# Roots ahead of the norms, scale and bias on GpSimd, gates' product freed, and gathers cut into steps, in a two-layer diffusion backbone

## The chip, the cores and the metric

The kernel runs on one NeuronCore of one Trainium2 chip. The metric is the device time of one launch in microseconds (us), the median of three runs. The engines are TensorE (PE; its weight loads are shown apart as PEld), VectorE (DVE), ScalarE (ACT), GpSimd (POOL) and the DMA queue that SyncE issues (SP).

## The reference

One inference step of a backbone with two layers, width 1024, on 128 prompt tokens and 128 sample tokens. Each layer is:

```
h = x*(1+scale1)+shift1                # scale, shift, gate from SiLU(cond) @ w_ada
y = mixer(h)                           # one projection in; HGRN2 and mLSTM branches, both directions;
                                       # their gates; y = (sig(gA)*(yA@WA) + sig(gB)*(yB@WB)) @ W_out
x = LayerNorm(alpha*x + gate1*y)       # ((x-mu)*rsqrt(var+eps))*g + b
h = x*(1+scale2)+shift2
f = SwiGLU(h), width 2816  (layer 0);  top-2-of-8 mixture of SwiGLU experts, width 2816  (layer 1)
x = LayerNorm(alpha*x + gate2*f)
```

All matrices are fp32. There are four norms. The first three are followed by a modulated copy (layer 0's feed-forward, layer 1's mixer, layer 1's experts); "inner norms" are the first and the second, whose g and b the change touches.

## The kernel before, in words

**Products.** Each weight tile is read by DMA into a staging tile (`ws`, in the expert stage also `mws`), ScalarE casts it to its high part (`wh`, `mwh`), VectorE subtracts to get the low part (`wl`, `mwl`), and TensorE makes three products: high by high, low by high, high by low. Activations are split the same way (`hTh` and `hTl`). `split` does this for the dense stages; it also holds back the low part of a few tiles with `held`, until work of the norm has been issued. Nearly every matrix product is recorded under line 56, nearly every two-input VectorE operation under line 52, so groups are told apart by tile names.

**Modulation.** `ada_quad` multiplies the conditioning (`actT`) with tiles of w_ada (`wa`, two slots) into the bank `adq`. Most of the 48 quads are spread over the two mixers and the feed-forward by the list `todo`, and stand between blocks of other products.

**A norm.** `residual` adds the gated product to x in halves of 512 columns; `layer_norm` takes the statistics of one block of 128 tokens, `inverse_dev` takes a root on ScalarE (line 400) and one Newton step on VectorE (line 402), and a scaled subtraction on VectorE (line 469) leaves the normalised block in `z`, without g and b. `modulate` turns `z` through TensorE (line 414) and scales it on ScalarE (line 420) or, for one quarter, on VectorE (line 423); g and b of the norm are folded into this scale and bias. `hT_part` splits the result. `between` puts a quad of the modulation between the transposes of the two blocks. Only the next residual needs x itself, so `affine` makes x = z*g + b later: two VectorE instructions for each block and each half, 8 for each inner norm. In the first norm they are entries of `todo`, in the second they follow the split of the activations; both are tied to `last_split`. The rows g and b of the second norm (`nrow`) lie in the two slots of `wa`.

**The mixer's gates.** `gates` in `mixer` loads 32 columns of weights (`gwh`, `gwl`) and multiplies them with the activations; its first product is tied behind a place noted in `grow["after"]`.

**The experts.** They run in pairs (`experts`). For each pair `gather` picks the tokens by a product with a 0/1 matrix `sel`: four steps of 16 products, for two row blocks each, then ScalarE copies the bank to `xh` and VectorE subtracts into `xl` (line 1388), then TensorE turns `sel` in four transposes. xh and xl have one pair of buffers, so the new tokens overwrite those that the running pair reads. Gathers 1 to 3 are called between the first two matrices of an odd expert and its third one, and each step takes a bank from `bank`, which has three buffers and serves the experts' products; `gbank` is one bank more, used for transposes of the activations (line 1452).

**Order.** The instructions of each engine stand in the order that a planner gives them from a simulated timeline of its own. `tc.high_priority()` lifts what is inside it, `tc.issue_after(i)` keeps what is inside it behind instruction i.

**Stages on the profiled run, us.** Layer 0 mixer to 422; product out and first norm to 452; feed-forward to 650; second norm to 663; layer 1 mixer to 1044; product out and third norm to 1080; router and first gather to 1089; experts to 1893; last norm to 1911.

Of the kernel before, what the change touches and what calls it, by code (L numbers as in the profile page):

```python
# [41 lines left out]
def backbone(ctx, tc, x_prompt, x_sample, c, state_hgrn, state_mlstm_C, state_mlstm_n, state_mlstm_m,  # L42
# [22 lines left out]

    eps = const.tile([128, 1], F32, name="eps")
    V.memset(eps, LN_EPS)
    ident = const.tile([128, 128], F32, name="ident")
# [123 lines left out]

    staged = []
    held = []

    def split(st, shape):
        hi = wp.tile(shape, F32R, tag="wh", name="wh", bufs=3)
        S.copy(hi, st)  # L198
        lo = wp.tile(shape, F32R, tag="wl", name="wl", bufs=3)
        with tc.issue_after(held.pop(0)) if held else nullcontext():  # L200
            tt(lo, st, hi.bitcast(F32), ALU.subtract)
        return hi, lo
# [122 lines left out]
    def ada_quad(l, c4, kt, halves=None):  # L325
# [5 lines left out]
        for g in (2, 3, 0, 1):  # L331
            with tc.high_priority(), tc.issue_after(end) if g < 2 else nullcontext():
                end = mm(ps[32 * g:32 * g + 32], actT[:, kt, :], halves[g // 2][:, g % 2], kt == 0, kt == KT - 1,
                         (0, 32 * g))
# [45 lines left out]
    def rsqrt(pool, src, n, mul, eps):  # L380
# [12 lines left out]
        return y  # L393

    def inverse_dev(pool, var):

        v = pool.tile([128, 1], F32, tag="rs_v", name="rs_v", bufs=2)
        y = pool.tile([128, 1], F32, tag="rs_y", name="rs_y", bufs=2)
        t = pool.tile([128, 1], F32, tag="rs_t", name="rs_t", bufs=2)
        act(t, var, AF.Sqrt, bias=eps)  # L400
        V.tensor_scalar(v, var, -0.5, -0.5 * LN_EPS, op0=ALU.mult, op1=ALU.add)
        V.reciprocal(y, t)
        V.tensor_scalar(t, y, y, v, op0=ALU.mult, op1=ALU.mult)
        V.tensor_scalar(y, t, 1.5, y, op0=ALU.add, op1=ALU.mult)
        return y

    def modulate(src, gs, bs, hm, between):

        for tr in range(2):
            for q4 in range(2):  # L410
# [6 lines left out]
                for k in range(4):  # L417
                    kt = q4 * 4 + k
                    if not tr or q4:
                        last_act[:] = [act(hm[:, kt, tr], ps[:, k], AF.Identity, bias=bs[:, kt, tr:tr + 1],  # L420
                                           scale=gs[:, kt, tr:tr + 1]).ins]
                    else:
                        last_mod[:] = [V.tensor_scalar(hm[:, kt, tr], ps[:, k], gs[:, kt, tr:tr + 1],
                                                       bs[:, kt, tr:tr + 1], op0=ALU.mult, op1=ALU.add).ins]
# [3 lines left out]
    def modulated_parts(pool, tag, src, gs, bs, between=lambda end: keep_warm(12, end)):  # L428
# [3 lines left out]
        lo = ht.tile([128, KT, 256], F32R, tag="hTl", name="hTl", bufs=1)  # L432
        modulate(src, gs, bs, hm, between)
        for q in range(4):
            hT_part(hm, hi, lo, q)
        return [(hi[:, k], lo[:, k]) for k in range(KT)]

    def hT_part(hm, hi, lo, q):
        s = slice(2 * q, 2 * q + 2)
        f = hm[:, s].rearrange("p k r t -> p (k r t)")  # L440
        S.copy(hi[:, s].rearrange("p k t -> p (k t)"), f)
        last_split[:] = [V.tensor_tensor(lo[:, s].rearrange("p k t -> p (k t)"), f,
                                         hi[:, s].bitcast(F32).rearrange("p k t -> p (k t)"), op=ALU.subtract).ins]

    last_split = []

# [38 lines left out]

    def affine(dst, src, gb, tr, q4):

        o = slice(512 * q4, 512 * q4 + 512)
        tt(dst[:, tr, o], src[:, tr, o], gb[0][:, o], ALU.mult)
        tt(dst[:, tr, o], dst[:, tr, o], gb[1][:, o], ALU.add)  # L490

    QUARTERS = [(tr, q4) for tr in range(2) for q4 in range(2)]


    def mixer(l, rhs, mx, sm, hp, mp, quads):
# [13 lines left out]
        def gates():  # L509
            gh, gl = load_gate_w(W)  # L510
            pg = mp.tile([32, 256], F32, tag="mp", name="pg")
            for kt in range(KT):
                rh, rl = rhs[kt]
                with nullcontext() if kt else tc.issue_after(grow.pop("after")):
                    mm(pg, gh[:, kt], rh, kt == 0, False)
# [447 lines left out]
    def mix_out(l, mrhs, pool, tags, obank, spare, bufs=1):  # L963
        z, ng = x, None
        if l == 0:
            z = slot8([128, 2, D], "z")
        banks = [gemm_tm(w_out[l], 512 * q4, 512, mrhs, obank, 1 + 3 * q4, spare) for q4 in range(2)]
        with tc.issue_after(staged[0]):
# [93 lines left out]
    with ExitStack() as es:  # L1062
# [16 lines left out]
        for i in range(1, KT):  # L1079
            todo.append((1, 0, i))  # L1080
        def late_affine(tr, q4, z=z, ng=ng):
            with tc.issue_after(last_split[0]):
                affine(x, z, ng, tr, q4)

        todo += [lambda tr=tr, q4=q4: late_affine(tr, q4) for tr, q4 in QUARTERS]
        keep_warm(4)

# [4 lines left out]
        with tc.high_priority():  # L1092
            rhs = modulated_parts(fx, "hm", z, gs, bs, between)
        held[:] = [last_mod[0], last_split[0], last_split[0]]
        gTh = fx.tile([128, 22, 256], F32R, name="gTh")
        gTl = fx.tile([128, 22, 256], F32R, name="gTl")

        for f0 in range(0, DFF, 512):
# [6 lines left out]
            for i, b in enumerate(gemm_fm(ffn_w3[0], f0, n, rhs, bank=fbank)):  # L1105
                s = slice(f0 // 128 + 2 * i, f0 // 128 + 2 * i + 2)
                t_ = ts[i]
                tt(t_, t_, b, ALU.mult)
                S.copy(gTh[:, s], t_)
                tt(gTl[:, s], t_, gTh[:, s].bitcast(F32), ALU.subtract)  # L1110
        gb = gate_rows(fx, "gb", 0, 1)
        ng = [norm_row(wp, "wa", ap, 2) for ap in (ln2_g[0], ln2_b[0])]
# [16 lines left out]
    def hT1(mx):  # L1129
        with tc.high_priority():  # L1130
            parts = modulated_parts(mx, "AQ", z, gs, bs)
        held[:] = [last_mod[0], last_split[0], last_split[0]]
        with tc.issue_after(last_split[0]):
            for tr, q4 in QUARTERS:
                affine(x, z, ng, tr, q4)
        return parts
# [218 lines left out]
    def experts(first_slot):  # L1355
# [5 lines left out]
        def gather(p2):  # L1361
# [12 lines left out]
            if not first_slot and p2 == 0:  # L1374
                banks = [pe.tile([128, 2, 256], F32, tag="acc", name="acc", bufs=3) for _ in range(3)]
                banks.append(adp.tile([128, 2, 256], F32, tag="ad", name="acc"))
                for k2, ps in zip(range(0, KT, 2), banks):
                    part(ps, k2, hh, True, False)
            for k2 in range(0, KT, 2):
                if banks:  # L1380
                    ps = banks[k2 // 2]
                else:
                    ps = bank([128, 2, 256])
                    part(ps, k2, hh, True, False)
                part(ps, k2, hl, False, True)
                o = slice(k2, k2 + 2)
                S.copy(xh[:, o], ps)
                done = V.tensor_tensor(xl[:, o], ps, xh[:, o].bitcast(F32), op=ALU.subtract).ins  # L1388
            ps = gbank([128, 2, 2, 128])
            for tr in range(2):  # L1390
                for i in range(2):
                    PE.transpose(ps[:, i, tr], sel[:, tr, i].bitcast(F32), ident)
            selT = ms.tile([128, 2, 2, 128], F32R, tag="selT", name="selT", bufs=2)
            S.copy(selT, ps)
            return sel, selT, xh, xl, done

# [11 lines left out]
        if not first_slot:  # L1408
            with tc.issue_after(nxt[4]):
                V.tensor_reduce(most, pm, axis=AX.X, op=ALU.max)  # L1410
                V.tensor_copy(most_i, most)
            behind.append(nxt[4])
            late.append(nc.values_load(most_i[0:1, 0:1], min_val=0, max_val=256))
        for p2 in range(NE // 2):
            sel, selT, xh, xl, _ = nxt
            for i in range(2):
# [41 lines left out]
                if i and p2 + 1 < NE // 2:  # L1458
                    nxt = gather(p2 + 1)
                if e == NE - 1:  # L1460
                    out = ms.tile([128, 2, D], F32, tag="e8", name="out", bufs=2)
                for q4 in range(2):
                    o = slice(512 * q4, 512 * q4 + 512)
                    yb = bank([128, 512])
                    for kt, wh, wl in blocks([moe_w2[0, e]], 22, 512 * q4, 512):
                        gh, gl = gT[kt]
                        mm(yb, gh, wh, kt == 0, False)
# [65 lines left out]
```

## Time and profile before

| what | value |
| --- | --- |
| time, median of 3 runs | 1909.88 us (1909.39 to 1910.23) |
| the profiled execution | 1913.11 us, its span 1911.4 us |
| mean granted TensorE clock | 0.990 of full speed |
| PE busy | 1842.6 us (96%) |
| PEld busy | 1572.2 us (82%) |
| DVE busy | 1473.4 us (77%) |
| ACT busy | 1187.9 us (62%) |
| POOL busy | 21.3 us (1%), 51 instructions |
| DMA | 500.88 MB, mean 262 GB/s |

The span runs from the first to the last instruction of the core; the time of an execution also has what lies around it. Busy times include waits inside a pipelined instruction only as far as the profile models them. A full granted clock is 2.4 GHz; a share of 0.5 is the other level, 1.2 GHz, and values between are means over a stretch.

### The profile page before, as it was taken

What the parts mean: (1) busy time and instruction counts of PE and PEld (TensorE: products, weight loads), DVE (VectorE), ACT (ScalarE), POOL (GpSimd) and SP (SyncE); (2) the same over time, 40 slices, a digit from 0 to 9 for tenths busy, and PEclk for the clock granted to TensorE, in tenths of its full rate; (3) what the DMA queues carried; (4) which work ended last, traced back from release to release, by engine and by line L of the source; (5) the groups of instructions that cost most, each with busy time, mean ns of one, the idle gap of its engine ahead of it and who ended that gap; (6) DMA issues with size and microseconds to landing.
All of it is one profiled execution on the core that took longest, in us unless ns stands there. A gap on an engine that the chain in (4) does not pass through costs nothing.

```text
span 1911.4 us, 30874 instructions
## 1 busy us (share of the span) xinstructions
PE 1842.6 (96%) x11846; PEld 1572.2 (82%) x11846; DVE 1473.4 (77%) x2179; ACT 1187.9 (62%) x1531; POOL 21.3 (1%) x51
## 2 busy tenths in 40 slices
PE   7999999998999899999999999999999999999996
PEld 4877889996998688788999787888887888788884
DVE  3587598676455658869957798989888898889887
ACT  4547555644444445665564587777776777677773
POOL 0000000000000000000000000000000000000000
PEclk9999999999999999999999999999999999999998
DMA  9866845567756585775555989999998999999993
GB/s 315 259 228 203 269 142 160 157 198 277 230 170 194 162 286 194 244 220 149 149 161 172 361 297 346 363 323 366 349 349 312 358 350 343 307 350 352 348 342 128
DMA packets 273579, 500.88 MB, mean 262 GB/s; under 512 B 17044, under 2 KB 56552, under 8 KB 273424
## 3 DMA queue, kind: packets, MB, share of 16 engines
q1 hardware_dynamic: 273424, 498.83, 78.0%
q8 instruction: 95, 1.56, 0.3%
q14 instruction: 60, 0.49, 0.1%
HBM read 493.45 MB, written 5.32 MB: 261 GB/s over the span
## 4 chain that ended last, share of the span: by engine, by line
PE 83%; DMA 9%; DVE 3%; ACT 2%; issue 1%; SPq 1%; DVEq 0%; ACTq 0%
PE mm L56 62%; PE fp L56 9%; DMA wa<-in_w_ada_dram 6%; PE adq L56 2%; PE pl L56 2%; PE acc L56 1%; PE pn L56 1%; DMA ws<-in_ffn_w_dram 1%; DVE wl L52 1%; PE g L1452 1%; DVE mwl L52 1%; PE pqk L56 1%; DMA ws<-in_w_in_dram 1%; PE po L56 1%; ACT wh L198 1%
## 5 line engine op out<-in xcount | busy, mean ns | idle before, releaser
L52 DVE TENSOR_TENSOR mwl<-mws,mwh 128x1024 fp32r<-128x1024 f32 x432 | 516.8, 1223 | 52.3 <-ACT mwh L1319 48.3
L1319 ACT CAST mwh<-mws 128x1024 fp32r<-128x1024 f32 x432 | 445.8, 1052 | 117.1 <-PE mm L56 109.1
L52 DVE TENSOR_TENSOR wl<-ws,wh 128x1024 fp32r<-128x1024 f32 (+1 forms) x275 | 331.4, 1207 | 189.9 <-ACT wh L198 184.8
L198 ACT CAST wh<-ws 128x1024 fp32r<-128x1024 f32 (+1 forms) x275 | 284.7, 1036 | 308.8 <-PE mm L56 149.1
L56 PE MATMUL mm<-hTh,wh 128*128 128x256 f32 x1024 | 293.8, 289 | 4.6 <-ACT wh L198 2.5
L56 PE MATMUL mm<-hTl,wh 128*128 128x256 f32 x1024 | 293.0, 287 | 1.7 <-DVE hTl L52 1.0
L56 PE MATMUL mm<-hTh,wl 128*128 128x256 f32 x1024 | 291.7, 288 | 2.4 <-DVE wl L52 2.4
L56 PE MATMUL mm<-mwh,xh 128*128 128x512 f32 x704 | 278.8, 396 | 0.0
L56 PE MATMUL mm<-mwl,xh 128*128 128x512 f32 x704 | 277.5, 399 | 0.9 <-DVE mwl L52 0.8
L56 PE MATMUL mm<-mwh,xl 128*128 128x512 f32 x704 | 278.4, 396 | 0.0
L56 PEld LDWEIGHTS mm<-hTh,wh 128*128 128x128 f32 x1024 | 196.4, 192 | 10.3 <-ACT wh L198 2.7
L56 PEld LDWEIGHTS mm<-hTh,wl 128*128 128x128 f32 x1024 | 195.3, 192 | 10.5 <-issue 5.1
L56 PEld LDWEIGHTS mm<-hTl,wh 128*128 128x128 f32 x1024 | 196.8, 192 | 8.6 <-issue 4.2
L56 PEld LDWEIGHTS mm<-mwl,xh 128*128 128x128 f32 x704 | 132.3, 188 | 32.3 <-DVE mwl L52 2.0
L56 PEld LDWEIGHTS mm<-mwh,xl 128*128 128x128 f32 x704 | 132.3, 188 | 31.8 <-DVE xl L1388 0.4
L56 PEld LDWEIGHTS mm<-mwh,xh 128*128 128x128 f32 x704 | 132.3, 188 | 30.0
L56 PE MATMUL mm<-mwh,gh 128*128 128x512 f32 x352 | 139.4, 397 | 1.5 <-ACT gt__12538 L1448 1.5
L56 PE MATMUL mm<-mwh,gl 128*128 128x512 f32 x352 | 139.4, 397 | 0.0
L56 PE MATMUL mm<-mwl,gh 128*128 128x512 f32 x352 | 138.8, 396 | 0.5 <-DVE mwl L52 0.5
L52 DVE TENSOR_TENSOR mwl<-ws,mwh 128x1024 fp32r<-128x1024 f32 x74 | 89.9, 1223 | 16.3 <-ACT mwh L1319 15.6
L56 PE MATMUL fp<-hTh,wh 128*128 128x256 f32 x352 | 100.7, 287 | 0.0
L56 PE MATMUL fp<-hTl,wh 128*128 128x256 f32 x352 | 100.1, 285 | 0.0
(600 smaller groups left out, 3119.4 us busy)
## 6 DMA issues: line engine op xcount, KB each, us to landing
mws<-in_moe_w_dram SPq DMA_DIRECT2D x202, 1024.0 KB
ws<-in_w_in_dram SPq DMA_DIRECT2D x160, 512.0 KB
wa<-in_w_ada_dram SPq DMA_DIRECT2D x96, 512.0 KB
ws<-in_moe_w_dram SPq DMA_DIRECT2D x70, 512.0 KB
ws<-in_ffn_w_dram SPq DMA_DIRECT2D x62, 512.0 KB
mws<-in_moe_w_dram SPq DMA_DIRECT2D x28, 512.0 KB
ws<-in_w_branch_a_dram SPq DMA_DIRECT2D x16, 512.0 KB
ws<-in_w_branch_b_dram SPq DMA_DIRECT2D x16, 512.0 KB
```

Source lines behind the costliest of these rows:

```text
L52: V.tensor_tensor(out, a, b, op=op)
L56: return PE.matmul(out, lhsT, rhs, start=start, stop=stop, skip_group_check=True, **kw).ins
L198: S.copy(hi, st)
L1319: S.copy(h, t_)
L1452: PE.transpose(ps[:, j], t_[:, j * 128:j * 128 + 128], ident)
```

## The change

It has four parts. (A) In front of each of the first three norms a root of a constant tile (eps squared) is issued behind an earlier cast, and its result is the bias of the norm's roots; the scalings of the upper columns are issued behind the norm's last root so far; from the first norm on, the quads' products for the scale groups are issued behind the last transpose of the latest modulated copy. (B) `affine` is made of GpSimd instructions over whole rows of 1024 columns, 4 for each inner norm, called right behind the modulated copy. (C) In layer 0 the gates' product is no longer tied to a place; in layer 1 the load and split of its weights is issued behind the last high part of the activations. (D) `gather` gives its four steps and the transposes of `sel` back as a list; for gathers 1 to 3 one entry is taken out in front of blocks 4, 8, 12, 16 and 20 of the 22 blocks of the odd expert's third matrix, first half, and each step's bank is `gbank`.

```
-    eps = const.tile([128, 1], F32, name="eps")
-    V.memset(eps, LN_EPS)
+    eps2 = const.tile([128, 1], F32, name="eps2")
+    V.memset(eps2, LN_EPS * LN_EPS)
+    eps_now = []
...
     def split(st, shape):
         hi = wp.tile(shape, F32R, tag="wh", name="wh", bufs=3)
-        S.copy(hi, st)
+        last_cast[:] = [S.copy(hi, st).ins]
...
         for g in (2, 3, 0, 1):                                  # in ada_quad
-            with tc.high_priority(), tc.issue_after(end) if g < 2 else nullcontext():
+            with tc.high_priority(), tc.issue_after(end if g < 2 else ada_after[0]) if g < 2 or ada_after else nullcontext():
...
+    root, ada_after = [], []
+
     def inverse_dev(pool, var):
...
-        act(t, var, AF.Sqrt, bias=eps)
+        root[:] = [act(t, var, AF.Sqrt, bias=eps_now[0]).ins]
...
+    def root_ready(after):
+
+        eps_now[:] = [base.tile([128, 1], F32, tag="rs_0", name="rs_0", bufs=1)]
+        with tc.issue_after(after):
+            act(eps_now[0], eps2, AF.Sqrt)
...
                     if not tr or q4:                            # in modulate
-                        last_act[:] = [act(hm[:, kt, tr], ps[:, k], AF.Identity, bias=bs[:, kt, tr:tr + 1],
-                                           scale=gs[:, kt, tr:tr + 1]).ins]
+                        with tc.issue_after(root[0]) if q4 else nullcontext():
+                            last_act[:] = [act(hm[:, kt, tr], ps[:, k], AF.Identity, bias=bs[:, kt, tr:tr + 1],
+                                               scale=gs[:, kt, tr:tr + 1]).ins]
...
         modulate(src, gs, bs, hm, between)                      # in modulated_parts
+        ada_after[:] = last_turn
...
-        S.copy(hi[:, s].rearrange("p k t -> p (k t)"), f)       # in hT_part
+        last_high[:] = [S.copy(hi[:, s].rearrange("p k t -> p (k t)"), f).ins]
...
-    def affine(dst, src, gb, tr, q4):
-
-        o = slice(512 * q4, 512 * q4 + 512)
-        tt(dst[:, tr, o], src[:, tr, o], gb[0][:, o], ALU.mult)
-        tt(dst[:, tr, o], dst[:, tr, o], gb[1][:, o], ALU.add)
+    def affine(dst, src, gb, tr):
+
+        G.tensor_tensor(dst[:, tr], src[:, tr], gb[0], op=ALU.mult)
+        G.tensor_tensor(dst[:, tr], dst[:, tr], gb[1], op=ALU.add)
...
         def gates():
-            gh, gl = load_gate_w(W)
+            with tc.issue_after(last_high[0]) if l else nullcontext():
+                gh, gl = load_gate_w(W)
...
-                with nullcontext() if kt else tc.issue_after(grow.pop("after")):
+                with tc.issue_after(grow.pop("after")) if l and not kt else nullcontext():
...
-        banks = [gemm_tm(w_out[l], 512 * q4, 512, mrhs, obank, 1 + 3 * q4, spare) for q4 in range(2)]
+        banks = []                                              # in mix_out
+        for q4 in range(2):
+            banks.append(gemm_tm(w_out[l], 512 * q4, 512, mrhs, obank, 1 + 3 * q4, spare))
+            if not q4:
+                root_ready(last_cast[0])
...
-        def late_affine(tr, q4, z=z, ng=ng):                    # first norm
-            with tc.issue_after(last_split[0]):
-                affine(x, z, ng, tr, q4)
-
-        todo += [lambda tr=tr, q4=q4: late_affine(tr, q4) for tr, q4 in QUARTERS]
...
         held[:] = [last_mod[0], last_split[0], last_split[0]]
+        for tr in range(2):
+            affine(x, z, ng, tr)
...
-                S.copy(gTh[:, s], t_)                           # feed-forward
+                last_cast[:] = [S.copy(gTh[:, s], t_).ins]
                 tt(gTl[:, s], t_, gTh[:, s].bitcast(F32), ALU.subtract)
+        root_ready(last_cast[0])
...
         held[:] = [last_mod[0], last_split[0], last_split[0]]   # second norm
-        with tc.issue_after(last_split[0]):
-            for tr, q4 in QUARTERS:
-                affine(x, z, ng, tr, q4)
+        for tr in range(2):
+            affine(x, z, ng, tr)
...
-            for k2 in range(0, KT, 2):                          # in gather
-                if banks:
-                    ps = banks[k2 // 2]
-                else:
-                    ps = bank([128, 2, 256])
+            def step(k2):
+                ps = banks[k2 // 2] if banks else gbank([128, 2, 256])
+                if not banks:
                     part(ps, k2, hh, True, False)
                 part(ps, k2, hl, False, True)
                 o = slice(k2, k2 + 2)
                 S.copy(xh[:, o], ps)
-                done = V.tensor_tensor(xl[:, o], ps, xh[:, o].bitcast(F32), op=ALU.subtract).ins
...
+            def places():
+                ps = gbank([128, 2, 2, 128])
...
+            steps = [lambda k2=k2: step(k2) for k2 in range(0, KT, 2)] + [places]
+            if not p2:
+                while steps:
+                    steps.pop(0)()
+            return sel, selT, xh, xl, done, steps
...
                 if i and p2 + 1 < NE // 2:
                     nxt = gather(p2 + 1)
+                    steps = nxt[5]
...
                     for kt, wh, wl in blocks([moe_w2[0, e]], 22, 512 * q4, 512):
+                        if steps and kt and kt % 4 == 0:
+                            steps.pop(0)()
```

## Rows read from the trace of the kernel before

**Rows 1.** The page, part 4: the chain that ended last, by engine.

```profile
PE 83%; DMA 9%; DVE 3%; ACT 2%; issue 1%; SPq 1%; DVEq 0%; ACTq 0%
```

**Rows 2.** Waits of PE: engine, line, waited for, us, times, longest.

```profile
PE adq L56 <- DMA wa<-in_w_ada_dram: 12.7, 14, 1.9
PE mm L56 <- DVE xl L1388: 7.3, 2, 3.6
...
PE mm L414 <- DVE z L469: 3.4, 3, 1.8
...
PE mm L56 <- DVE wl L52: 2.4, 2, 2.0
```

**Rows 3.** Waits of the DMA queue SP: the longest sum.

```profile
SPq L1280 <- DVE mwl L52: 614.9, 281, 10.2
```

**Rows 4.** Timeline of PE at the gathers: start, us, instruction, count, wait.

```profile
1252.88 0.63 PE L56 MATMUL mm<-sel,hhl 128*128 128x256 f32 x4
1253.34 0.63 PE L56 MATMUL mm<-sel,hhh 128*128 128x256 f32 x4
...
1458.23 1.22 PE L56 MATMUL mm<-sel,hhh 128*128 128x256 f32 x4 [3.64 <-DVE xl L1388]
...
1461.62 0.38 PE L1452 MATMUL g<-ident,gt__15194 128*128 128x128 f32 x2
...
1662.44 0.99 PE L56 MATMUL mm<-sel,hhh 128*128 128x256 f32 x4 [3.62 <-DVE xl L1388]
```

**Rows 5.** Timeline of DVE at the second gather.

```profile
1457.48 1.28 DVE L1388 TENSOR_TENSOR xl<-mm,xh 128x512 fp32r<-128x512 f32 x2
```

**Rows 6.** Windows: stretch, length, busy us by engine, PEclk, DMA, GB/s.

```profile
650.00:700.00 50.00, 42.21 (x312) 36.03 (x311) 33.40 (x60) 25.28 (x47) 0.11 (x1) 0.97 0.71 220
669.00:674.00 5.00, 4.52 (x25) 4.52 (x26) 5.00 (x7) 0.00 (x0) 0.00 (x0) 0.66 0.83 258
1451.00:1468.00 17.00, 13.36 (x68) 11.44 (x67) 12.88 (x15) 10.72 (x15) 0.00 (x0) 0.90 0.81 292
```

**Rows 7.** Line 400 (roots): its table loads, and who waited for it.

```profile
L400 ACT ACT_TABLE_LOAD  x4: 1283/1283/1283, 439.0 to 1894.5; - x4
...
  DVE rs_y L402: 10.5, 6
```

**Rows 8.** Timeline of PE in the first norm.

```profile
442.00 1.11 PE L414 MATMUL mm<-ident,z 128*128 128x128 f32 x8 [1.31 <-DVE z L469]
...
449.84 1.94 PE L56 MATMUL adq<-wa,actT 128*32 128x512 f32 x8 [1.03 <-DMA wa<-in_w_ada_dram]
```

**Rows 9.** Timeline of PE in and after the second norm.

```profile
653.08 1.11 PE L414 MATMUL mm<-ident,z 128*128 128x128 f32 x8 [0.25 <-DVE z L469]
...
658.73 1.05 PE L56 MATMUL adq<-wa,actT 128*32 128x512 f32 x4 [1.86 <-DMA bb<-in_b_in_dram]
...
669.48 0.58 PE L56 MATMUL mm<-hTh,wl 128*128 128x256 f32 x1 [1.98 <-DVE wl L52]
...
672.63 0.40 PE L56 MATMUL mm<-hTh,wh 128*128 128x256 f32 x1
```

**Rows 10.** Timeline of ACT in the second norm.

```profile
654.47 2.91 ACT L420 ACTIVATE hm<-mm,bs,gs 128x128 f32<-128x128 f32 x8 [1.85 <-PE mm L414]
```

**Rows 11.** Timeline of ACT in the third norm.

```profile
1075.54 0.33 ACT L400 ACTIVATE rs_t<-ln_mv,eps 128x1 f32<-128x1 f32 x1
```

**Rows 12.** Timeline of DVE after the second norm.

```profile
665.79 2.50 DVE L52 TENSOR_TENSOR x<-z,nrow 128x512 f32<-128x512 f32 x4
```

**Rows 13.** Timeline of POOL and DVE in the layer 0 mixer.

```profile
176.67 0.41 POOL L841 TENSOR_SCALAR_AFFINE_SELECT w<-w 128x256 f32<-128x256 f32 x1 [14.02 <-PE adq L56]
...
341.27 1.23 DVE L52 TENSOR_TENSOR wl<-ws,wh 128x1024 fp32r<-128x1024 f32 x1 [1.58 <-ACT wh L198]
341.84 0.93 POOL L841 TENSOR_SCALAR_AFFINE_SELECT w<-w 128x256 f32<-128x256 f32 x1 [21.13 <-ACT w L840]
```

**Rows 14.** Timeline of the DMA queue SP after the second norm.

```profile
673.00 3.30 SPq L320 DMA_DIRECT2D wa<-in_w_ada_dram  x2
```

More of the change, by code (lines that the diff above doesn't have):

```diff
@@ L191, in stage @@
         return st
-    staged = []
+    staged, last_cast = [], []
     held = []
@@ L440, in hT_part @@
         f = hm[:, s].rearrange("p k r t -> p (k r t)")
-        S.copy(hi[:, s].rearrange("p k t -> p (k t)"), f)
+        last_high[:] = [S.copy(hi[:, s].rearrange("p k t -> p (k t)"), f).ins]
         last_split[:] = [V.tensor_tensor(lo[:, s].rearrange("p k t -> p (k t)"), f,
                                          hi[:, s].bitcast(F32).rearrange("p k t -> p (k t)"), op=ALU.subtract).ins]
-    last_split = []
+    last_split, last_high = [], []
     def gate_rows(pool, tag, l, which, bufs=1):
@@ L484, in norm_rows @@
         return gb[:, 0], gb[:, 1]
-    def affine(dst, src, gb, tr, q4):
-        o = slice(512 * q4, 512 * q4 + 512)
-        tt(dst[:, tr, o], src[:, tr, o], gb[0][:, o], ALU.mult)
-        tt(dst[:, tr, o], dst[:, tr, o], gb[1][:, o], ALU.add)
-    QUARTERS = [(tr, q4) for tr in range(2) for q4 in range(2)]
+    def affine(dst, src, gb, tr):
+        G.tensor_tensor(dst[:, tr], src[:, tr], gb[0], op=ALU.mult)
+        G.tensor_tensor(dst[:, tr], dst[:, tr], gb[1], op=ALU.add)
     def mixer(l, rhs, mx, sm, hp, mp, quads):
@@ L1387, in gather @@
                 S.copy(xh[:, o], ps)
-                done = V.tensor_tensor(xl[:, o], ps, xh[:, o].bitcast(F32), op=ALU.subtract).ins
[L1389 to L1392, printed above, removed]
-            selT = ms.tile([128, 2, 2, 128], F32R, tag="selT", name="selT", bufs=2)
-            S.copy(selT, ps)
-            return sel, selT, xh, xl, done
+                done[:] = [V.tensor_tensor(xl[:, o], ps, xh[:, o].bitcast(F32), op=ALU.subtract).ins]
+            def places():
+                ps = gbank([128, 2, 2, 128])
+                for tr in range(2):
+                    for i in range(2):
+                        PE.transpose(ps[:, i, tr], sel[:, tr, i].bitcast(F32), ident)
+                S.copy(selT, ps)
+            done = []
+            selT = ms.tile([128, 2, 2, 128], F32R, tag="selT", name="selT", bufs=2)
+            steps = [lambda k2=k2: step(k2) for k2 in range(0, KT, 2)] + [places]
[3 more added lines that the diff above has]
+            return sel, selT, xh, xl, done, steps
         def slot_weights(p2, sel):
@@ L1408, in experts @@
         if not first_slot:
-            with tc.issue_after(nxt[4]):
+            with tc.issue_after(nxt[4][0]):
                 V.tensor_reduce(most, pm, axis=AX.X, op=ALU.max)
                 V.tensor_copy(most_i, most)
-            behind.append(nxt[4])
+            behind.append(nxt[4][0])
             late.append(nc.values_load(most_i[0:1, 0:1], min_val=0, max_val=256))
         for p2 in range(NE // 2):
-            sel, selT, xh, xl, _ = nxt
+            sel, selT, xh, xl, _, steps = nxt
             for i in range(2):
```

## The prediction

> **What bounds the kernel now.** I read the chain of waits first [rows 1]. The reader is to see that 83% of the span is matrix products in a row and 9% transfers; VectorE and ScalarE hold only the seams. So an edit pays only where TensorE stands still, and the list of what it waited for gives the places [rows 2]: 14 waits for modulation weights, two for the low half of gathered tokens (xl), three for a normalised row block, two for the low half of a weight. The change leaves the first and aims at the other three. In the expert stage the DMA queue waits for buffers 281 times, 614.9 us in all [rows 3]: weights are issued when products free buffers, so a stall removed from TensorE there is not simply handed to the transfers.
>
> **The gathers.** Before the third matrix of experts 1, 3 and 5 the tokens of the next pair are gathered: four steps of 16 products, each into one of three shared banks. The planner runs two steps early, inside the last columns of the first two matrices. Their results may not leave the banks before that product is over, because they overwrite the tokens it reads. Third in line, step three finds no bank: TensorE stops for 3.64 us at the second gather and 3.62 us at the third, waiting for xl [rows 4]; VectorE reaches xl at 1457.48, behind weight splits [rows 5]. The products of the third matrix, whose weights are ready, stand behind the step in the queue. After the stop the granted clock is down: it averages 0.90 over 17 us [rows 6], so 0.2 of 17 us, 3.4 us, ran at 1.2 GHz. At the first gather four products step in 1253.34 − 1252.88 = 0.46 us; 16 would take 1.9 us, and at the second they took 1461.62 − 1458.23 = 3.39 us [rows 4]. The lower clock thus costs 1.5 us each time. The stalls are worth 3.64 + 3.62 + 2 × 1.5 = 10.3 us.
>
> The change lets blocks 0 to 3 of the third matrix go first, then one step per four blocks, in a bank of its own. By block 4 the old tokens are free. What is late next: that bank is single, and the last columns' transposes use it before step one; their two copies take at most 0.64 us each by the row of xl [rows 5], 1.28 us for two of twice their width, so up to 1.3 us may show at each of three gathers. Four blocks of product lie between two steps, so the later copies are covered. The cost lies between 0 and 3.9 us; I take 1.1, because blocks 0 to 3 cover most of it. Gathers: −9.2 us, bounds −10.3 and 0 (the stall may only move).
>
> **The roots.** A table load of 1.283 us sits in front of the first root of each norm, and VectorE waits 10.5 us over six roots [rows 7]. The change puts a tiny root after earlier casts, so that the load falls into ScalarE's idle time; the cover is the product then running, and without it 1.6 us would delay a cast. It also holds the scalings of the upper columns behind the second root.
>
> First norm: the transposes waited 1.31 us for the normalised block, and TensorE has nothing else there [rows 8]. The load's 1.28 us comes off. Before the next product stands a modulation quad that waits 1.03 us for its weights [rows 8]; they are issued when the quad before frees the buffers, which moves up too. So 1.3 us stay, and what the second root gains vanishes in that wait. Bounds −2.0 and 0.
>
> Second norm: the first transposes waited only 0.25 us [rows 9], so the load hardly counts for block 0. For block 1 it does: its residual is queued behind block 0's normalisation and comes 1.28 us earlier. Its root stood behind eight scalings of 2.91 us [rows 10]; behind four it is 1.45 us earlier. The quad that held TensorE for 1.86 + 1.05 us ahead of the last transposes [rows 9] is sent behind them, and the gate weights' cast, which would stop ScalarE in front of the scalings once these move up, goes behind the last split. 1.28 + 1.45 = 2.7; I take −2.6, bounds −2.9 and 0.
>
> Third norm: TensorE is still in the product, so the load is worth nothing for block 0. The second root, at 1075.54 [rows 11], comes up to 1.45 us earlier, but the router's products stand before the last transposes and want the scalings now held back. I take −0.9, bounds −1.4 and 0. The roots: −1.3 − 2.6 − 0.9 = −4.8 us.
>
> **The inner norms' scale and bias.** Sixteen VectorE instructions go; the first four of the second norm take 2.50 us in front of a weight split [rows 12]. TensorE stops 1.98 us for that split [rows 9], and the 15 products after it take 672.63 − 669.48 = 3.15 us. The clock averages 0.66 over 5 us there [rows 6], so 0.68 of them, 3.4 us, ran at 1.2 GHz: half of the 3.15 us, 1.6, is the clock's. So −3.6 us, bounds −3.6 and 0. In the first norm nobody waited for them: nothing.
>
> GpSimd takes over with eight instructions of twice the width. No row shows a two-input instruction there. One input and 256 columns take 0.41 us [rows 13]; four times the width is 1.6 us, the lower bound, two inputs 3.3 us. Started inside a 1.23 us split of VectorE it takes 0.93 us and ends with that split [rows 13]: GpSimd is held off. If it moved only in the third of the time that the 67% busy VectorE leaves [rows 6], one would take 10 us, the upper bound. I take 4 us, since the row nearest to a split more than doubles: four from 652 end at 668, ahead of the 673.0 at which the old ones let the queue issue the next weights [rows 14]. The rows shared with those weights are thus free earlier; nothing is lost.
>
> By the Trainium skill (GPSIMD Engine Reference, section "Performance versus the Vector engine") VectorE should keep such work, as GpSimd takes 1.96 times as long; its 4497 ns for 2048 columns make an estimate of 2.25 us for one here, and four would end at 661. No run here shows that figure; the sum would be the same by it, as both ends lie before 673.
>
> VectorE may also be held off by GpSimd. On block 1's chain a two-input step (0.63 us, a quarter of the 2.50 in [rows 12]) and the normalisation can each wait for half an instruction, 2 us by my price: 4 us in a norm, 8 in two, against 0 from the split that stayed at 1.23 us beside GpSimd [rows 13]. I take 2.5, nearer to the row.
>
> **The gates.** In layer 0 the product is no longer tied to a place, in layer 1 a cast moves (counted above). TensorE does not wait for either: 0, bounds ±0.5.
>
> **Sum.** −9.2 − 4.8 − 3.6 + 2.5 = −15.1 us. The profiled execution took 1913.1 us, 1.7 of it outside its span, and would take 1898.0. It stands 3.2 us above the median of the runs; from 1909.9 the same saving gives 1894.8, in round figures 1895.
>
> **Rivals.**
> *The gathers alone pay.* GpSimd's share of the port costs what roots and norms bring (8 against 8.4): 1909.9 − 9.2 = 1900.7. For it: the held-off row. Against: VectorE's split is not longer there. The same page of the Trainium skill (section "Key points") says the two engines contend when VectorE has two SBUF inputs; the trace agrees for GpSimd's side, at 0.93 against 0.41 us.
> *The gathers do not spread.* The planner orders the queues by its own simulated times and already ran steps early; if it bunches them again, or the single bank stops step one for as long as xl did, that term is 0 and −5.9 remains: 1904.0. For it: the early steps of before. Against: with one bank two steps cannot be outstanding.
> *Slower.* GpSimd's four instructions keep the norm's rows, whose slots the modulation weights need; the weights of layer 1 stand behind these in the DMA queue. Each microsecond past 673 delays them by about one. It decides when it eats 15.1 us, at 688, nine a piece from 652. At the upper bound of 10 us they end at 692: 4 us slower, 1914. Against: VectorE loses its own share of that work.
>
> **Chances.** Forecast 0.52 (from −11 to −17.5); gathers alone 0.24; no spread 0.12; slower by the rows 0.06; 0.06 for a better sum still, mostly with no port cost. The range 1887 to 1904.5 holds the first two, half of the third and most of the last. The likeliest case by itself spans 1892 to 1899. Within 0.2% (3.8 us, about what this kernel's measurement can tell) falls the tail of the third and part of the fourth: faster 0.87, same 0.08, slower 0.05.
>
> **What would show it.** Right: no wait for xl, and steps of the gather between blocks of the third matrix at 0.46 us per four; no table load between aggregate and root; GpSimd busy some 30 us in two places and done before TensorE's second weight block; transposes of the second norm ahead of the quad. Wrong: a stop ahead of step one; two-input instructions of VectorE longer than 0.63 or 1.23 us beside GpSimd; modulation weights issued later than the last split. The prediction fails mostly if the planner puts new waits elsewhere, as every queue is ordered anew.

## The result, and the profile after

The changed kernel takes 1897.55 us, the median of 5 runs (1892.16 to 1897.62), beside 1910.23 us for the kernel before in 5 runs of the same comparison; the ratio is 0.9911, 95% interval [0.9893, 0.9929]. The time lies 2.6 us from the forecast of 1895 and inside its range. The saving is 12.7 us by the two medians and 17 us (14 to 20) by the ratio; the forecast was 15.1. The span of the profiled execution is 1895.8 us.

The page of the kernel after, busy times and the chain of waits (beside [rows 1]):

```profile
PE 1835.7 (97%) x11846; PEld 1568.2 (83%) x11846; DVE 1465.9 (77%) x2163; ACT 1176.2 (62%) x1534; POOL 40.6 (2%) x59
...
PE 85%; DMA 8%; DVE 4%; ACT 1%; issue 1%; SPq 0%; DVEq 0%; ACTq 0%
```

What TensorE waited for in the kernel after (total, times, longest):

```profile
PE adq L56 <- DMA wa<-in_w_ada_dram: 9.1, 13, 1.8
PE mm L423 <- DVE z L480: 5.4, 3, 3.0
...
PE mm L56 <- DVE hTl L453: 2.9, 1, 2.9
...
PE fp L56 <- DVE hTl L453: 2.7, 1, 2.7
...
PE mm L56 <- DVE wl L52: 0.5, 1, 0.5
```

Beside [rows 2], the 7.3 us for xl and most of the wait for wl are gone. In their place stand two new waits for hTl, 5.6 us together, and the wait for the normalised block has grown from 3.4 to 5.4 us.

The second gather after, on TensorE, and the window around it:

```profile
1454.25 0.64 PE L56 MATMUL g<-sel,hhh 128*128 128x256 f32 x4
...
1462.66 0.63 PE L56 MATMUL g<-sel,hhh 128*128 128x256 f32 x4
```

```profile
1443.00:1490.00 47.00, 47.00 (x225) 38.73 (x224) 41.39 (x41) 35.90 (x43) 0.00 (x0) 1.00 1.00 360
```

The steps now stand 8.4 us apart between blocks of the third matrix. TensorE is busy for the whole 47 us and the granted clock is 1.00, where it was 0.90 over 17 us in [rows 6].

ScalarE before and in the first norm, after:

```profile
411.48 1.28 ACT L414 ACT_TABLE_LOAD   x1
...
430.35 1.05 ACT L199 CAST wh<-ws 128x1024 fp32r<-128x1024 f32 x1 [1.52 <-DMA ws<-in_ffn_w_dram]
431.30 0.29 ACT L403 ACTIVATE rs_t<-ln_mv,rs 128x1 f32<-128x1 f32 x1
```

The table load of [rows 7] has moved 20 us ahead of the root, into the product.

GpSimd, VectorE and TensorE in the first norm, after:

```profile
433.70 2.36 POOL L499 TENSOR_TENSOR x<-z,ngb 128x1024 f32<-128x1024 f32 x1 [105.28 <-PE mm L423]
436.13 2.67 POOL L500 TENSOR_TENSOR x<-x,ngb 128x1024 f32<-128x1024 f32 x1
439.77 2.36 POOL L499 TENSOR_TENSOR x<-z,ngb 128x1024 f32<-128x1024 f32 x1 [0.97 <-DVE z L480]
442.21 3.21 POOL L500 TENSOR_TENSOR x<-x,ngb 128x1024 f32<-128x1024 f32 x1
```

```profile
434.02 2.58 DVE L953 SCALAR_TENSOR_TENSOR z<-x,z 128x512 f32<-128x512 f32 x1
436.63 0.69 DVE L470 BATCH_NORM_STATS2 ln_st<-z 128x6 f32<-128x512 f32 x1
...
441.27 1.94 DVE L52 TENSOR_TENSOR wl<-ws,wh 128x1024 fp32r<-128x1024 f32 x1
443.14 4.64 DVE L453 TENSOR_TENSOR hTl<-hm,hTh 128x512 fp32r<-128x512 f32 x4
```

```profile
439.29 1.18 PE L423 MATMUL mm<-ident,z 128*128 128x128 f32 x8 [2.95 <-DVE z L480]
...
446.03 0.58 PE L56 MATMUL fp<-hTl,wh 128*128 128x256 f32 x1 [2.66 <-DVE hTl L453]
```

The second norm's stop on TensorE, after:

```profile
662.88 0.43 PE L56 MATMUL mm<-hTl,wh 128*128 128x256 f32 x1 [2.95 <-DVE hTl L453]
```

The window on TensorE behind the first norm's stop, after:

```profile
446.00:453.00 7.00, 6.97 (x36) 6.00 (x37) 5.06 (x6) 1.05 (x1) 0.00 (x0) 0.61 0.52 180
```

This is the part that the sum had wrong. The residual step of VectorE (0.69 us undisturbed) starts at 434.02, inside a GpSimd instruction that ends at 436.06, and ends at 436.60, 0.54 us behind it: it was held until GpSimd's instruction was over. GpSimd's next one, which begins while that step still runs, takes 2.67 instead of 2.36 us. The four splits of hTl (2.50 us before) start at 443.14 and end at 447.78, 2.36 us behind the end of GpSimd's last one at 442.21 + 3.21 = 445.42. The statistics at 436.63, which read one tensor, are not held. TensorE pays: block 1's transposes wait 2.95 us at 439.29 (1.8 at most in [rows 2]), the first product with hTl waits 2.66 us at 446.03, and the products of the next 7 us run at a mean granted clock of 0.61. The second norm shows the same, with 2.35 us for the residual step, 4.63 for the splits and a stop of 2.95 us for hTl at 662.88.

### The profile page after: what moved, and what is told of

Its sections match the earlier page's. It is cut to its first block, busy times and chain, and to the rows that moved or that the text cites. A ratio compares the mean times of both kernels' runs of the same rounds, so it can differ in the third digit from the quotient of the medians.

```text
span 1895.8 us, 30792 instructions
## 1 busy us (share of the span) xinstructions
PE 1835.7 (97%) x11846; PEld 1568.2 (83%) x11846; DVE 1465.9 (77%) x2163; ACT 1176.2 (62%) x1534; POOL 40.6 (2%) x59
## 4 chain that ended last, share of the span: by engine, by line
PE 85%; DMA 8%; DVE 4%; ACT 1%; issue 1%; SPq 0%; DVEq 0%; ACTq 0%
PE mm L56 64%; PE fp L56 9%; DMA wa<-in_w_ada_dram 6%; PE adq L56 2%; PE pl L56 2%; PE acc L56 1%; PE g L56 1%; DMA ws<-in_ffn_w_dram 1%; PE pn L56 1%; DVE mwl L52 1%; PE g L1468 1%; DVE wl L52 1%; PE po L56 1%; PE pqk L56 1%; DMA ws<-in_w_out_dram 1%
## 5 line engine op out<-in xcount | busy, mean ns | idle before, releaser
L1329 ACT CAST mwh<-mws 128x1024 fp32r<-128x1024 f32 x432 | 437.5, 1051 | 82.7 <-PE mm L56 75.7
L56 PE MATMUL fp<-hTh,wl 128*128 128x256 f32 x352 | 100.6, 286 | 0.0
```

Source lines behind the costliest of these rows:

```text
L56: return PE.matmul(out, lhsT, rhs, start=start, stop=stop, skip_group_check=True, **kw).ins
L1329: S.copy(h, t_)
```

## The experiments

A, B, C and D name the parts as the change does: roots, scale and bias, gates, gathers. Each kernel was timed beside the kernel before, whose medians were 1914.2, 1914.2 and 1913.6 us in the three groups. Single executions of one kernel differ by some us, so a profile alone doesn't decide about less.

**Each part alone** (kernel before with that part of the diff):

Gathers: 

> Only part D of the change (the stepped gathers) put into the kernel before. Theory 1 (terms as read from the trace after): the two stops for xl go and nothing else moves, -9 us (-8 to -10.5) against the kernel before; no wait of a product for xl. The prediction's own terms say the same, -9.2. Rival 2 (every change reorders the queues, so the stages ahead of the experts move too): the first transposes of the first norm start more than 3 us away from 442.0.

Gates: 

> Only part C (the gates' product not tied in layer 0; in layer 1 the cast of the gates' weights behind the last high part). Theory 1: this is what moved the first norm from 442.0 to 433.0; so the first transposes start at 432 to 436 and about 9 us are gained there, of which at the end of the run something between 4 and 9 us is left. The prediction's term: 0 +- 0.5. Rival 2 (the queues of layer 0 are reordered by whatever is changed): 0 here, and shifts of the first norm in the other runs of this group as well.

Roots: 

> Only part A (roots ahead of the norms, scalings behind the last root, quads behind the last transpose). The prediction's term: -4.8 us (-1.3, -2.6, -0.9 in the three norms). Theory 1: the same, -3 to -5, as no GpSimd instruction disturbs it: no table load between the aggregate and the root, and each norm from its first transposes to the next product 1 to 3 us shorter. Rival 2: the sum is hidden by shifts of over 3 us in the mixers.

Scale and bias: 

> Only part B (scale and bias of the inner norms on GpSimd). Theory 1 (VectorE instructions with two inputs in SBUF wait for the end of the GpSimd instruction that runs): one residual step and the four splits of hTl take 2 us longer each time in both norms, TensorE stops 2 to 3 us ahead of the first product with hTl and runs its next 15 to 30 products at 1.2 GHz; +3 to +8 us against the kernel before, although the stop of 1.98 us for the weight split goes. The prediction's terms: -3.6 + 2.5 = -1.1. Rival 2: a shift of the first norm's start too.

Measured, with the saving as ratio minus 1 times the median of before: D alone 0.9936 [0.9912, 0.996], −12 us (−17 to −8); C alone 0.9976 [0.9963, 0.999], −4.6 us (−7.1 to −1.9); A alone 0.9967 [0.995, 0.9985], −6.3 us (−9.6 to −2.9); B alone 1.0011 [0.9996, 1.0027], +2.1 us (−0.8 to +5.2). A, C and D pay. B's time shows no gain, though the loss is less than the +3 to +8 us expected. Its profile shows where it loses: the residual step takes 2.59 and 2.36 us in the two norms; hTl's splits are held in the first (4.45 us), in the second the splits of gates' and product weights ahead of them (1.53 and 2.09 us); and from the last product ahead of a norm to the first with hTl it takes 15.6 and 14.7 us, the kernel before 12.9 and 12.6.

The profile of D alone shows the gathers' share more sharply than its time: from the first product of the experts to the end of the span it takes 813.0 us (1089.5 to 1902.5), the kernel before 822.2. That is the −9.2 forecast. But its first norm starts at 438.7 instead of 442.0, although ahead of the experts no queue has its instructions in another order. So part of the 9.0 us by which that norm starts earlier after the change (433.0) belongs to the single execution, and expectation 2 of the first run came true for another reason than it gave.

**The changed kernel once more**, and **without B** (parts A, C and D; `affine` in quarters on VectorE as before):

> The changed kernel once more, unchanged, for a second profile and as the yardstick of this group. Theory 1 (part of the 9.0 us by which the first norm started earlier is a matter of one execution, since the kernel with the gathers alone has the same order up to the experts as the kernel before and started that norm 3.3 us earlier): the first transposes start up to 4 us away from 433.0, while the norms from there to the next product and the gathers repeat within 0.5 us. Rival 2 (the 9.0 us belong to the order of the queues): 433.0 within 1 us. The time against the kernel before: 0.989 to 0.993 by both.

> The change without part B: scale and bias of the inner norms stay on VectorE in quarters, as before. Theory 1 (two-input instructions of VectorE wait out GpSimd's): no step of 2.3 us or more among the residuals, hTl's four splits take 2.5 instead of 4.6 us in both norms, the stops of 2.7 and 3.0 us ahead of the first product with hTl go; the stop for the weight split after the second norm (about 2 us, and the low clock behind it) comes back; 2 to 5 us faster than the changed kernel. The prediction's terms: 1.1 us slower than the changed kernel (it loses -3.6 and gains 2.5).

Again: 0.9908 [0.9891, 0.9925], 1897.75 us; the first norm starts at 433.6, within 1 us as rival 2 has it, and the stops ahead of the first product with hTl are 1.63 and 2.94 us. Without B: 0.9884 [0.9866, 0.9903], 1894.84 us, 2.9 us faster by the medians and 4.6 by the ratios, though the two intervals overlap. Both stops for hTl are gone and hTl's splits take 2.50 us again; from the last product ahead of the second norm to the first with hTl it takes 8.8 instead of 12.9 us. The stop for the weight split is back. Without B, on TensorE:

```profile
660.85 0.39 PE L56 MATMUL mm<-hTh,wl 128*128 128x256 f32 x1 [1.97 <-DVE wl L52]
```

So B removes this stop and puts longer ones in its place. In sum the prediction's terms had the sign the other way.

**GpSimd's work issued later.** The edit, at both calls:

```
+        with tc.issue_after(last_split[0]):
             for tr in range(2):
                 affine(x, z, ng, tr)
```

> The changed kernel with GpSimd's eight instructions issued behind the last split of the norm's activations. Theory 1: the residual step and hTl's splits are short again (0.7 and 2.5 us) and the stops ahead of the first product with hTl go, 2.7 and 3.0 us and the low clock behind them; VectorE's weight splits of 1.23 us that follow now take 2 to 3.5 us, of which TensorE sees one stop of at most 2 us in each norm; 2 to 6 us faster than the changed kernel. Rival (the modulation weights that need the rows' slots are late): the queue issues them 8 to 10 us later behind the second norm, TensorE waits for them, and the time is the changed kernel's or up to 4 us more.

0.9907 [0.989, 0.9924], the changed kernel's time. The edit did not do what it says. GpSimd in this kernel:

```profile
434.03 2.36 POOL L499 TENSOR_TENSOR x<-z,ngb 128x1024 f32<-128x1024 f32 x1 [104.00 <-PE mm L423]
```

It starts as early as in the kernel after, and in this trace every engine and the DMA queue have their instructions in the same order as there. So `issue_after` held nothing back here, where the instruction to wait for is VectorE's and those inside are GpSimd's. Neither theory was tested; the run is in effect the changed kernel a third time, with stops of 1.87 and 2.94 us ahead of the first product with hTl.

**GpSimd's work in short pieces.**

```
+        for q in range(4):
+            o = slice(256 * q, 256 * q + 256)
+            G.tensor_tensor(dst[:, tr, o], src[:, tr, o], gb[0][:, o], op=ALU.mult)
+            G.tensor_tensor(dst[:, tr, o], dst[:, tr, o], gb[1][:, o], op=ALU.add)
```

> The changed kernel with GpSimd's eight instructions of 1024 columns cut into thirty-two of 256. Theory 1 (the two engines take turns instruction by instruction): a two-input instruction of VectorE waits for at most one short one, 0.6 us; the residual step takes at most 1.4 us instead of 2.58, but each of hTl's four splits may wait once, so these stay at 4 us or more; the gain is 0 to 3 us against the changed kernel. Rival (they share the port by bytes, so that the time lost depends on columns and not on instructions): residual step and splits take as long in sum as in the changed kernel, 2.6 and 4.6 us.

0.9903 [0.9883, 0.9923], 1896.48 us: no difference in time that can be told. The rows do tell. VectorE in its first norm:

```profile
435.21 1.19 DVE L955 SCALAR_TENSOR_TENSOR z<-x,z 128x512 f32<-128x512 f32 x1
436.44 0.69 DVE L470 BATCH_NORM_STATS2 ln_st<-z 128x6 f32<-128x512 f32 x1
...
438.50 1.70 DVE L480 TENSOR_SCALAR z<-z,ln_mv,rs_y 128x512 f32<-128x512 f32 x2
...
443.51 4.35 DVE L453 TENSOR_TENSOR hTl<-hm,hTh 128x512 fp32r<-128x512 f32 x4 [0.91 <-ACT hTh L452]
```

The residual step waits for one short instruction (1.19 instead of 2.58 us), and four splits in a row wait four times (4.35). That is taking turns by instructions, theory 1; sharing by bytes would have left 2.6 us. The normalisation, with one input, is held too, 1.70 instead of 1.00 us, and the statistics are not.

TensorE's stops ahead of the first product with hTl are gone (0.00 and 0.23 us), and the two norms take 11.7 and 9.8 us, in the changed kernel's two profiles 15.4 and 14.1, 12.9 and 12.9. The time is still the changed kernel's, because the gain is lost again behind the second norm: layer 1's mixer takes 409.0 us between its norms, the changed kernel's 402.2 and 403.7. GpSimd's last piece on the second norm's rows ends 7.3 us behind the first product with hTl there, the changed kernel's last instruction 0.6 us ahead of it.

**The kernel before once more**, and **without C**:

> The kernel before once more, unchanged, for a second profile. Theory 1 (the start of the first norm is partly a matter of one execution): its first transposes start at 436 to 441, not at 442.0, so only some 4 to 6 of the 9.0 us belong to the change. Rival 2 (all of it belongs to the order of the queues): 442.0 within 1 us. By both the two stops for xl (3.6 us each) and the stop of about 2 us for the weight split after the second norm repeat.

> The change without part C: the gates' product in layer 0 tied to its place again, the cast of the gates' weights in layer 1 free again. Theory 1 (the tied product delays the gates' chain in the first mixer, so that casts of weights come late behind it; the gates alone gave -4.6 us): 2 to 6 us slower than the changed kernel, the difference there by the first norm, and a stop of TensorE for a cast of over 1 us between 150 and 175 us comes back. The prediction's term: within 0.5 us of the changed kernel.

Before again (one run, 1911.92 us): the first norm starts at 438.4, the stops for xl repeat at 3.64 and 3.61 us, but the stop for the weight split does not. On TensorE:

```profile
666.55 0.39 PE L56 MATMUL mm<-hTh,wl 128*128 128x256 f32 x1 [0.48 <-DVE wl L52]
```

It is 0.48 us where [rows 9] has 1.98. The term of −3.6 us priced a stop that differs from execution to execution; what B saves behind the second norm is read from the stages below.

Without C: 0.9943 [0.9927, 0.996], 1902.06 us, slower than the changed kernel by 4.3 us by the medians and by 6 to 7 by the ratios; its interval overlaps that of the first timing of the changed kernel by 0.0002 and does not meet that of the second. Alone the gates gave 4.6 us, so the two agree within their intervals. The transposes of the last result of the gates' chain, without C and then in the second profile of the changed kernel (137.19 in the first):

```profile
147.31 0.22 PE L585 MATMUL pc<-ident,t 8*128 8x8 f32 x1
```

```profile
138.19 0.22 PE L586 MATMUL pc<-ident,t 8*128 8x8 f32 x1
```

The gates' product starts at 53 instead of 61 us, their chain over ScalarE and VectorE ends 9 to 10 us earlier, and TensorE's wait for a cast at 159 (1.28 us; 2.53 and 1.10 in the two profiles of the kernel before) is gone. The first norm starts at 432.1 to 436.4 in the eight profiles with C (mean 434.3) and at 435.1 to 442.0 in the six without (mean 438.9): 4.6 us, the same again. Layer 1's moved cast shows nothing in that layer's mixer: it takes 402.6 us between its norms without C, and 402.2 and 403.7 with it.

**GpSimd's work behind the last split by data.**

```
+    def behind_split():
+
+        t_ = base.tile([128, 8], F32, tag="rs_g", name="rs_g", bufs=1)
+        with tc.issue_after(last_split[0]):
+            return G.tensor_copy(t_, last_lo[0]).ins            # reads the last part of hTl
...
+        with tc.issue_after(behind_split()):                    # at both calls
+            for tr in range(2):
+                affine(x, z, ng, tr)
```

> The changed kernel with a small GpSimd copy that reads the last part of hTl in front of the scale and bias, so that GpSimd really waits for the last split of the activations. Theory 1: the residual step takes 0.7 and hTl's four splits 2.5 us again, from the last product before a norm to the first with hTl it takes some 13 us in the first norm and 9 in the second, as with part B undone; the weight splits behind are held off instead, one of them up to 2.4 us each time, of which at most one stop of 2 us in each norm is seen; 2 to 6 us faster than the changed kernel. Rival (the rows' slots come free late): modulation weights behind the second norm are issued after 673 us, TensorE waits 2 us or more for them, and nothing is gained.

0.991 [0.9891, 0.9929]: nothing gained, the rival. The norms are at least as short as theory 1 says, 11.4 and 8.9 us. But behind the second one VectorE and GpSimd take turns over the weight splits, and the modulation weights come late: GpSimd is done with the rows 15.5 us behind the first product with hTl, and the queue issues the weights for that slot then. VectorE, then TensorE, in this kernel:

```profile
654.14 2.63 DVE L52 TENSOR_TENSOR gwl<-gws,gwh 128x256 fp32r<-128x256 f32 x1
...
656.69 10.07 DVE L52 TENSOR_TENSOR wl<-ws,wh 128x1024 fp32r<-128x1024 f32 x3
```

```profile
674.35 1.08 PE L56 MATMUL adq<-wa,actT 128*32 128x512 f32 x8 [2.27 <-DMA wa<-in_w_ada_dram]
...
720.36 1.94 PE L56 MATMUL adq<-wa,actT 128*32 128x512 f32 x8 [2.64 <-DMA wa<-in_w_ada_dram]
```

The second mixer takes 413.3 us between its norms, the changed kernel 402.2 and 403.7. This is the mechanism of the prediction's slower rival, at a smaller price.

**VectorE again, one place later** (parts A, C and D; the first norm as in the kernel without B, the second against it):

```
-        with tc.issue_after(last_split[0]):
-            for tr, q4 in QUARTERS:
-                affine(x, z, ng, tr, q4)
...
-    todo += [None, None] + [(1, 1 + i // 8, i % 8) for i in range(16)]
+    todo += [lambda tr=tr: late_affine2(tr) for tr in range(2)]   # both halves of block tr, behind last_split
+    todo += [(1, 1 + i // 8, i % 8) for i in range(16)]
```

> The change without part B, and the second norm's scale and bias, on VectorE, issued one place later, behind two more weight splits. Theory 1 (the stop for a weight split after the second norm is queue order alone): the stop of 1.97 us at 660.85 in the kernel with part B undone goes, and with it the low clock behind it; 2 to 4 us faster than that kernel, 4 to 7 faster than the changed one. Rival (VectorE has no room there, or the modulation weights wait for the rows): the stop moves to a later split or to the modulation weights, and the time is that of the kernel with part B undone.

0.9867 [0.9845, 0.989], 1889.1 us: faster than both kernels; its interval ends just below that of the changed one (0.989 beside 0.9891 and 0.9893), 8 us by the ratios where 4 to 7 were expected. VectorE behind the second norm, and the window there:

```profile
655.98 2.35 DVE L52 TENSOR_TENSOR wl<-ws,wh 128x1024 fp32r<-128x1024 f32 x2
658.25 2.49 DVE L52 TENSOR_TENSOR x<-z,nrow 128x512 f32<-128x512 f32 x4
```

```profile
653.00:690.00 37.00, 33.66 (x265) 29.35 (x266) 27.56 (x42) 18.97 (x32) 0.00 (x0) 1.00 0.83 271
```

The two weight splits stand ahead of the scale and bias, no wait for wl is left there, and the granted clock is 1.00, although TensorE waits 1.85 us for modulation weights at 665.54. Against the kernel with B merely undone this is 5.7 us by the medians and 3.3 by the ratios; those two intervals overlap. Of the 4.0 us between the two spans 2.7 lie in layer 1's mixer.

## Why the prediction was right, point by point

Where the time went, by stages of the traces (us; the mean of two profiles for the kernels before and after, one profile for each other; the norms are counted up to the first product with hTl; "pieces" has GpSimd's work in short pieces, "behind" has it behind the last split by data):

| stage | before | after | without B | pieces | behind | split first |
| --- | --- | --- | --- | --- | --- | --- |
| start to the end of norm 1 | 450.5 | 446.3 | 446.7 | 444.8 | 442.4 | 446.6 |
| feed-forward | 199.8 | 202.7 | 200.0 | 200.2 | 198.9 | 198.9 |
| norm 2 | 12.4 | 12.9 | 8.8 | 9.8 | 8.9 | 8.8 |
| layer 1's mixer and product out | 407.7 | 403.0 | 407.2 | 409.0 | 413.3 | 404.5 |
| norm 3 to the first expert | 18.1 | 17.6 | 17.6 | 17.6 | 17.6 | 17.6 |
| experts to the end of the span | 822.3 | 813.2 | 813.1 | 813.0 | 813.1 | 813.1 |

**Gathers, −9.2: right in mechanism and size.** The table has 9.1, no product waits for xl, the steps lie between blocks and no stop stands ahead of step one. D's own timing allows it (−17 to −8). Of it the first gather gives almost nothing: counted from the first product of the experts, expert 1's third matrix starts 4.9 us earlier with D alone, but the steps have only moved into that product, and at the next expert's third matrix 0.5 us are left. The other two gathers, which had the stops, give 5.4 and 4.7 us by the same count, and 1.2 us are lost again in the last expert. The prediction reads [rows 3] as weights issued when products free buffers; the row names VectorE's splits. No term changes by that.

**Roots, −4.8: right.** From the last product before to the first behind, A alone takes 11.4, 10.0 and 17.6 us in the three norms, the kernel before 12.9 and 12.8, 12.6 and 12.3, and 18.1: −1.4, −2.5 and −0.5 for the −1.3, −2.6 and −0.9 of the sum. The time of A alone (−9.6 to −2.9) agrees. Layer 1's mixer takes 410.4 us in that profile, more than before, so what of the −2.5 outlasts it isn't settled by one profile.

**Inner norms, −3.6 + 2.5 = −1.1: the mis-sized term is the 2.5.** The price of the port took half an instruction of waiting at two places; the rows show a wait for all that is left of GpSimd's instruction, at three places in each norm: 1.9, 0.7 and 2.1 us in the first, 1.7, 0.7 and 2.1 in the second. That is 9.2 us of VectorE, beyond the 8 us of the upper bound, and TensorE's two new stops for hTl of 2.66 and 2.95 us come of it, with a low clock behind each. With B norm 2 takes 12.9 to 13.3 us in the four profiles that also have A, without it 8.8 and 10.0 (without B, and A alone). GpSimd itself was priced at 4 us an instruction and takes 2.36 to 3.21.

The saving of 3.6 us came in size, but not where it was priced. The stop of 1.98 us is 0.48 in another execution, and the first 65 products of layer 1's mixer with hTl take about as long with B (29.6 to 31.3 us) as without it (28.8 to 30.3). Yet the whole mixer takes 402.2 to 404.8 us in the five profiles that have B as the change does, and 406.9 to 410.9 in the six that leave scale and bias as before, some 5 us less. The prediction put the earlier release of the rows at nothing ("nothing is lost"). In the kernel before the queue issues modulation weights into the second of these slots at 673.00, 8.9 us behind the first product with hTl; in the kernel after it does so 0.6 us ahead of that product:

```profile
662.31 0.33 SPq L321 DMA_DIRECT2D wa<-in_w_ada_dram  x1
```

From 30 to 130 us behind that product TensorE then waits 0.6 to 2.2 us for such weights in the five profiles, 3.5 to 4.0 in the six. The kernels that release the rows later than the changed one by GpSimd ("pieces", "behind") have the longer mixer. The rest of the 5 us isn't traced, and release isn't all of it: the kernel whose splits come first holds the rows 10.3 us past that product and takes 404.5.

By its own timing B costs +2.1 (−0.8 to +5.2), by its undoing 2.9 to 4.6 us; the sum had −1.1.

By the Trainium skill (GPSIMD Engine Reference, section "Performance versus the Vector engine") one such instruction was estimated at 2.25 us, and the undisturbed one of 2.36 agrees. By the Trainium skill (same page, section "Key points") VectorE's instructions contend with GpSimd in a two-port mode or with two inputs in SBUF; the residual step and the splits of hTl are of the second kind, and the traces agree (2.58 instead of 0.69 us and 4.64 instead of 2.50). No row here shows in which mode the held normalisation ran.

**Gates, 0 ± 0.5: wrong, −4.5.** The prediction looked at whether TensorE waits for the gates' product or cast, and it does not. The step that failed is the silent one that nobody else waits for it: the product's place fixed when the gates' chain on ScalarE and VectorE began, and the recurrences and weight casts queue behind that chain. The runs show the size twice, 4.6 us alone and 4.3 to 6.7 undone; through which of these queues most of it comes is argued from the moved rows, not separately tested.

The two misses have opposite signs, about −4.5 and +3 to +6, and nearly cancel: that the sum of −15.1 stands between the measured −12.7 (medians) and −17 (ratio times 1910.2), and beside −15.2 between the mean spans of two profiles each, is owed in part to that luck. Of the rivals, "the gathers alone pay" had the port's price nearer (8 us) and missed the gates as the sum did; the gathers did spread; the slower case's late modulation weights appeared only in kernels whose GpSimd work ends later, without making them slower than before.

## What to carry to other kernels

When work moves to GpSimd, look at which VectorE instructions with two inputs in SBUF run at the same time, and charge each the rest of a GpSimd instruction; and ask what its end lets go, as rows freed earlier by GpSimd went with a shorter stage behind them here, and rows freed later with a longer one. One place later on VectorE, behind the splits that TensorE needs next, was worth more here. Before an edit is costed at nothing because TensorE does not wait for it, follow the chain that it starts on the other engines. A single stop of 1 to 2 us between transfers and products may not be there in the next execution, so a term is better read from the length of the whole stage in several profiles than from one row.

## What was not expected of the hardware

A VectorE normalisation with one input in SBUF was held by GpSimd's short instructions (1.70 instead of 1.00 us for two), while statistics of one tensor beside the same instructions took their usual 0.69 us. After a stop of 2.66 us the mean granted clock was 0.61 over the next 7 us. In the kernel whose splits come first, with no stop over 1.9 us there, it stayed at 1.00.
